# A masked prefix sum of eight sequences: blocks planned from registers, or a gather by a table of units

## The chip, the cores and the metric

The kernel runs on one core of a Trainium2 chip. The metric is the device time of one execution in microseconds, first to last instruction, given as the median of several executions. Lower is better.

## What is computed

```
B, S, D = 8, 8192, 512          # x: 8 x 8192 x 512 fp32, lengths: 8 whole numbers, w: 512 x 512 fp32
mask = pos < lengths
cs = cumsum(x * mask, axis=1)
mid = cs[b, lengths[b] // 2, :]
out = mid @ w                   # 8 x 512
```

Only one row of each cumulative sum is used, so for sequence b the answer is the sum of its first n rows, with n = min(lengths // 2 + 1, lengths), times w. For the lengths of this draw (1138, 5379, 511, 4113, 1809, 7542, 7716, 1140), n is 570, 2690, 256, 2057, 905, 3772, 3859 and 571: 14,680 rows of 2 KB in all, 30.1 MB. They must be read from memory; the arithmetic is small. The lengths are known only on the chip, so the program must decide there which rows it reads.

## The kernel before

The row sum is a matrix product: a block of rows lies in SBUF with 128 partitions, and TensorE multiplies it by a matrix 128 x 8 that has ones in the column of the sequence, adding into `s_ps`. Four such products, each in its own column group of the array, take the four rows that a partition holds; the four groups are added up later by a product with `fold`.

SyncE issues all reads of x, and TensorE must know which of them there are. Each of the two loads all the lengths from memory into registers and works the row counts out there (`counts`, line 80, and the arithmetic of lines 83 to 85). Then come three passes.

- Whole blocks (lines 97 to 115): for each sequence, `whole_blocks` compares n with 512, 1024 and so on, and for each block that is full issues one 1 MB transfer in which every partition gets four consecutive rows, 8 KB. `xt` holds the blocks of two sequences; block k of sequence b waits (line 105) until the block k of sequence b-2 is summed. For this draw there are 26 blocks.
- Remainders (lines 121 to 153): what is left of each sequence, below 512 rows, is read by the binary digits of n: 256 rows (line 129, two rows or 4 KB a partition), 128 rows (line 136, 2 KB a partition), and the last up to 127 rows in a multiple of 32 (line 143). They go into `rem`, and the last piece is multiplied by `mask`, which VectorE makes of the lengths.
- The end: after a closing product (line 254) VectorE copies `s_ps` to SBUF (one copy of 128x512), TensorE folds and transposes it (line 261), VectorE copies, TensorE multiplies by w (line 268), VectorE copies, and four transfers write the output from two queues (lines 156 and 165).

ScalarE's queue loads lengths for VectorE and the whole of w (lines 161 and 162) at the start. GpSimd clears part of `rem` (line 169) and makes two index vectors. VectorE's helper `step` (line 182) runs one operation at a time, each waiting for the one before. Nothing here is reordered by a scheduler: each engine runs its list in the order written.

Of the kernel before, what the change touches and what calls it, by code (L numbers as in the profile page):

```python
# [8 lines left out]
I32 = mybir.dt.int32  # L9
ALU = mybir.AluOpType  # L10
ds = bass.ds
# [4 lines left out]
def kernel(  # L16
# [10 lines left out]


    nc = tc.nc
    ctx.enter_context(nc.allow_non_contiguous_dma(reason="lengths"))  # L30
    B, S, D = x.shape
    G = 4
    BLK = P * G
    NB = S // 2 // BLK
    KC = D // P
    STEP = 32
    xf = x.rearrange("b s d -> (b s) d")
# [12 lines left out]

    xt = sb("xt", [P, 2, NB, G, D])
    rem = sb("rem", [P, B, G, D])
    wt = sb("wt", [P, KC, D])
    lens = sb("lens", [P, 2 * B], I32)
    cnt = sb("cnt", [P, B], I32)
    cap = sb("cap", [P, B], I32)
    row = sb("row", [P, 1], I32)
    mask = sb("mask", [P, B, B])
    sel = sb("sel", [P, 2 * B - 1])
    zero = sb("zero", [1, D])  # L60
    fold_i = sb("fold_i", [P, B], I32)
    fold = sb("fold", [P, B])
# [5 lines left out]
    mf_ps = ps("mf_ps", [P, D])  # L68
    o_ps = ps("o_ps", [P, D])

    s_full = [[sem(f"full{b}_{k}") for k in range(NB)] for b in range(B)]
    s_rem = [[sem(f"rem{b}_{k}") for k in range(3)] for b in range(B)]
    s_free = [sem(f"free{b}") for b in range(B)]
    s_w, s_len, s_out = sem("w"), sem("len"), sem("out")
    s_pool, s_dve, s_pe = sem("pool"), sem("dve"), sem("pe")

    def counts(eng):

        regs = [eng.alloc_register(f"n_{eng.engine.name}_{i}") for i in range(2 * B)]
        eng.load(regs, lens_words)  # L80
        for b in range(B):
            length, n = regs[2 * b], regs[2 * b + 1]
            eng.reg_alu(n, length, 1, ALU.logical_shift_right)
            eng.reg_alu(n, n, 1, ALU.add)
            eng.reg_alu(n, n, length, ALU.min)
        return regs[1::2], regs[0]

    def whole_blocks(eng, n, body, k=0):
        if k < NB:
            with eng.If_cmp(n, BLK * (k + 1), "IS_GE"):  # L90
                body(k)
                whole_blocks(eng, n, body, k + 1)

    DVE_SEL, DVE_MASK = 3, 12

    block = ctx.enter_context(nc.Block(no_gpsimd_drain=True))

    @block.sync
    def _(sp):
        ns, t = counts(sp)  # L100

        def wait_free(b, k):

            if b >= 0:
                with sp.If_cmp(ns[b], BLK * (k + 1), "IS_GE"):  # L105
                    sp.wait_ge(s_free[b], k + 1)
                with sp.Else():
                    wait_free(b - 2, k)

        for b in range(B):  # L110
            def load_block(k):
                wait_free(b - 2, k)
                sp.dma_start(  # L113
                    out=xt[:, b % 2, k],
                    in_=x[b, k * BLK:(k + 1) * BLK].rearrange("(p g) d -> p g d", g=G),
                ).then_inc(s_full[b][k], 16)

            whole_blocks(sp, ns[b], load_block)

        def rows(b, first, count):  # L120
            return xf[ds(sp.snap(first) + b * S, count)]  # L121

        sp.wait_ge(s_pool, 1)
        for b in range(B):
            base = sp.alloc_register(f"base{b}")
            sp.reg_alu(t, ns[b], 256, ALU.bitwise_and)
            with sp.If_cmp(t, 1, "IS_GE"):
                sp.reg_alu(base, ns[b], ~(2 * 256 - 1), ALU.bitwise_and)
                sp.dma_start(  # L129
                    out=rem[:, b, 0:2],  # L130
                    in_=rows(b, base, 256).rearrange("(p g) d -> p g d", g=2),
                ).then_inc(s_rem[b][0], 16)
            sp.reg_alu(t, ns[b], 128, ALU.bitwise_and)
            with sp.If_cmp(t, 1, "IS_GE"):
                sp.reg_alu(base, ns[b], ~(2 * 128 - 1), ALU.bitwise_and)
                sp.dma_start(out=rem[:, b, 2], in_=rows(b, base, 128)).then_inc(s_rem[b][1], 16)  # L136
            sp.reg_alu(t, ns[b], 127, ALU.bitwise_and)
            sp.reg_alu(base, ns[b], ~127, ALU.bitwise_and)

            def load_last(lo, hi):  # L140

                if hi - lo == STEP:
                    sp.dma_start(out=rem[:hi, b, 3], in_=rows(b, base, hi)).then_inc(s_rem[b][2], 16)  # L143
                    return
                mid = (lo + hi) // 2
                with sp.If_cmp(t, mid, "IS_GT"):
                    load_last(mid, hi)
                with sp.Else():
                    load_last(lo, mid)

            with sp.If_cmp(t, 1, "IS_GE"):
                load_last(0, 128)

        sp.wait_ge(s_dve, DVE_MASK + 3)
        for j in range(0, 4, 2):
            sp.dma_start(out=out[:, j * P:(j + 1) * P], in_=o_sb[32 * j:32 * j + B]).then_inc(s_out, 16)
        sp.wait_ge(s_out, 64)

    @block.scalar
    def _(act):  # L160
        act.dma_start(out=lens[:], in_=lens_words.to_broadcast((P, 2 * B))).then_inc(s_len, 16)
        act.dma_start(out=wt[:], in_=w.rearrange("(kc p) d -> p kc d", p=P)).then_inc(s_w, 16)
        act.wait_ge(s_dve, DVE_MASK + 3)
        for j in range(1, 4, 2):
            act.dma_start(out=out[:, j * P:(j + 1) * P], in_=o_sb[32 * j:32 * j + B]).then_inc(s_out, 16)

    @block.gpsimd
    def _(pool):
        pool.memset(rem[:, :, 3], 0.0).then_inc(s_pool, 1)  # L169
        pool.iota(row[:], pattern=[[0, 1]], base=0, channel_multiplier=1)  # L170
        pool.iota(fold_i[:], pattern=[[-1, B]], base=128, channel_multiplier=1).then_inc(s_pool, 1)

    @block.vector
    def _(dve):
        done = 0

        def step(do, *args, **kw):

            nonlocal done
            if done:  # L180
                dve.wait_ge(s_dve, done)
            do(*args, **kw).then_inc(s_dve, 1)  # L182
            done += 1

        step(dve.memset, zero[:], 0.0)
        step(dve.memset, sel[:], 0.0)
        step(dve.memset, sel[:, B - 1:B], 1.0)
        assert done == DVE_SEL
        step(dve.memset, mask[:], 0.0)
        step(dve.memset, o_ps[:, :P], 0.0)  # L190
        dve.wait_ge(s_len, 16)
        step(dve.tensor_scalar, out=cnt[:], in0=lens[:, ::2], scalar1=1, scalar2=None,
             op0=ALU.logical_shift_right)
        step(dve.tensor_scalar, out=cap[:], in0=cnt[:], scalar1=1, scalar2=None, op0=ALU.add)
        step(dve.tensor_tensor, out=cnt[:], in0=cap[:], in1=lens[:, ::2], op=ALU.min)
        step(dve.tensor_scalar, out=cap[:], in0=cnt[:], scalar1=127, scalar2=None,
             op0=ALU.bitwise_and)
        dve.wait_ge(s_pool, 2)
        step(dve.tensor_tensor, out=mask[:].rearrange("p a b -> p (a b)")[:, ::B + 1], in0=cap[:],
             in1=row[:].to_broadcast((P, B)), op=ALU.is_gt)  # L200
        step(dve.tensor_scalar, out=cnt[:], in0=fold_i[:], scalar1=31, scalar2=None,
             op0=ALU.bitwise_and)
        step(dve.tensor_scalar, out=fold[:], in0=cnt[:], scalar1=0, scalar2=None, op0=ALU.is_equal)
        assert done == DVE_MASK
        dve.wait_ge(s_pe, 1)
        step(dve.tensor_copy, out=s_sb[:], in_=s_ps[:])
        dve.wait_ge(s_pe, 2)
        step(dve.tensor_copy, out=mf_sb[:].rearrange("p a b -> p (a b)"), in_=mf_ps[:, :KC * B])
        dve.wait_ge(s_pe, 3)
        step(dve.tensor_copy, out=o_sb[:], in_=o_ps[:, :P])  # L210

    @block.tensor
    def _(pe):
        ns, t = counts(pe)

        def add(j, weights, rows):

            return pe.matmul(s_ps[32 * j:32 * j + weights.shape[-1]], lhsT=weights, rhs=rows,  # L218
                             start=False, stop=False, skip_group_check=True,
                             tile_position=(0, 32 * j))  # L220

        pe.wait_ge(s_dve, DVE_SEL)
# [3 lines left out]
        for b in range(B):  # L226
            one = sel[:, B - 1 - b:2 * B - 1 - b]

            def add_block(k):
                pe.wait_ge(s_full[b][k], 16)  # L230
                for j in range(G):
                    mm = add(j, one, xt[:, b % 2, k, j])
                mm.then_inc(s_free[b], 1)

            whole_blocks(pe, ns[b], add_block)
# [66 lines left out]
```

## Time and profile before

| what | value |
|---|---|
| median of 3 executions | 101.29 us (100.38 to 101.92) |
| span of the profiled execution | 100.6 us |
| TensorE busy | 58.3 us |
| VectorE busy | 3.9 us |
| GpSimd busy | 4.0 us |
| bytes moved | 31.48 MB, mean 313 GB/s |
| 26 whole blocks, 1024 KB each | 12.8 us median from issue to landing |
| w, 1024 KB | 5.4 us from issue to landing |

The page gives time in microseconds from the first instruction. "SPq" is SyncE's queue, "ACTq" ScalarE's; a DMA row of a timeline shows how long the queue took to issue a transfer, not how long the data travelled. "PEld" is TensorE's load of weights. In a table of stages, "DMA share" is the mean busy share of the 16 DMA engines and the last number is what they moved. [...]

### The profile page before, as it was taken

The page shows a single profiled execution, that of the slowest core. Times are in us where ns is not written, and L with a number is a line of the kernel's source. Part 1 is how long each engine was busy: PE and PEld are TensorE (multiplying, and loading weights), DVE is VectorE, ACT ScalarE, POOL GpSimd, SP SyncE. Part 2 cuts the span into 40 slices and gives each one's busy share as a digit, 9 for nine tenths or more (in the row PEclk, how much of TensorE's full clock was granted, in tenths as well). Part 3 has the DMA queues.
Part 4 walks back from the last instruction along what each step waited for, and adds up shares of the span by engine and source line. Part 5 has one row for each costly group of instructions (what it writes and reads, how often), then busy time and mean ns, then how long its engine had stood idle before and what let it go on. Part 6 is the DMA issues. An engine that isn't in the chain of part 4 may idle for free.

```text
span 100.6 us, 1017 instructions
## 1 busy us (share of the span) xinstructions
PE 58.3 (58%) x296; PEld 8.3 (8%) x296; DVE 3.9 (4%) x15; POOL 4.0 (4%) x7
## 2 busy tenths in 40 slices
PE   0006177744763954199444767744755796996820
PEld 0000000000000100010000000000000111113700
DVE  3520000000000000000000000000000000002010
POOL 7800000000000000000000000000000000000000
PEclk9999999998555699755999555596555569998555
DMA  0836999999999999999999999999999995100000
GB/s 2 270 148 195 427 427 430 430 420 420 427 420 417 427 423 417 414 417 414 427 420 420 423 423 423 410 420 423 420 281 290 328 283 136 34 0 0 0 7 0
DMA packets 5786, 31.48 MB, mean 313 GB/s; under 512 B 816, under 2 KB 848, under 8 KB 2448
## 3 DMA queue, kind: packets, MB, share of 16 engines
q1 hardware_dynamic: 5072, 30.29, 76.3%
q10 hardware_dynamic: 704, 1.07, 3.2%
q8 instruction: 5, 0.08, 0.3%
q14 instruction: 5, 0.04, 0.1%
HBM read 31.33 MB, written 0.02 MB: 312 GB/s over the span
## 4 chain that ended last, share of the span: by engine, by line
DMA 41%; SPq 31%; issue 13%; PE 9%; DVE 1%
DMA xt<-in_x_dram 25%; DMA rem<-in_x_dram 16%; SPq L113 10%; SPq L143 6%; SPq L80 5%; PE s_ps L218 5%; SPq L129 3%; PE o_ps L268 2%; PE mf_ps L261 2%; SPq L105 1%; SPq L136 1%; PE s_ps L254 1%; SPq L90 1%; DVE s_sb L182 1%; SPq L121 1%
## 5 line engine op out<-in xcount | busy, mean ns | idle before, releaser
L218 PE MATMUL s_ps<-xt,sel 128*8 128x512 f32 x208 | 42.6, 905 | 28.6 <-DMA xt<-in_x_dram 23.4
L218 PEld LDWEIGHTS s_ps<-xt,sel 128*8 128x8 f32 x208 | 3.7, 91 | 67.5 <-DMA xt<-in_x_dram 58.0
L218 PE MATMUL s_ps<-rem,mask 128*8 128x512 f32 x14 | 8.0, 670 | 0.8 <-issue 0.8
L218 PE MATMUL s_ps<-rem,sel 128*8 128x512 f32 x18 | 6.6, 643 | 0.1
L224 PE MATMUL s_ps<-zero 1*32 1x512 f32 x8 | 1.9, 1056 | 7.3 <-issue 7.3
L182 DVE COPY s_sb<-s_ps 128x512 f32<-128x512 f32 x1 | 0.7, 692 | 85.8 <-PE s_ps L254 85.8
L169 POOL MEMSET rem<- 128x4096 f32 x1 | 3.5, 3512 | 0.5 <-SPq L40 0.5
L261 PE MATMUL mf_ps<-fold,s_sb 128*128 128x8 f32 x8 | 1.7, 340 | 0.8 <-DVE s_sb L182 0.8
L268 PE MATMUL o_ps<-wt,mf_sb 128*8 128x128 f32 x32 | 1.9, 416 | 0.3 <-DVE mf_sb L182 0.3
L261 PEld LDWEIGHTS mf_ps<-fold,s_sb 128*128 128x128 f32 x8 | 1.6, 298 | 1.7 <-DVE s_sb L182 1.7
L218 PEld LDWEIGHTS s_ps<-rem,mask 128*8 128x8 f32 x14 | 1.0, 97 | 6.0 <-issue 4.1
L268 PEld LDWEIGHTS o_ps<-wt,mf_sb 128*8 128x8 f32 x32 | 1.1, 126 | 0.7 <-DVE mf_sb L182 0.4
L254 PE MATMUL s_ps<-zero 1*32 1x512 f32 x8 | 1.1, 600 | 0.0
L218 PEld LDWEIGHTS s_ps<-rem,sel 128*8 128x8 f32 x18 | 0.6, 87 | 3.3 <-DMA rem<-in_x_dram 3.1
L182 DVE TENSOR_SCALAR cnt<-lens 128x8 int32<-128x8 int32 x1 | 0.8, 822 | 1.3 <-DMA lens<-in_lengths_dram 1.3
L224 PEld LDWEIGHTS s_ps<-zero 1*32 1x32 f32 x8 | 0.2, 136 | 7.3 <-issue 7.3
L182 DVE MEMSET zero<- 1x512 f32 x1 | 0.5, 485 | 1.1 <-PEq L286 1.1
L182 DVE COPY o_sb<-o_ps 128x128 f32<-128x128 f32 x1 | 0.3, 291 | 2.0 <-PE o_ps L268 2.0
L182 DVE TENSOR_SCALAR cap<-cnt 128x8 int32<-128x8 int32 x2 | 0.3, 172 | 0.1
L182 DVE COPY mf_sb<-mf_ps 128x32 f32<-128x32 f32 x1 | 0.2, 192 | 1.8 <-PE mf_ps L261 1.8
L254 PEld LDWEIGHTS s_ps<-zero 1*32 1x32 f32 x8 | 0.2, 102 | 0.9 <-issue 0.9
L182 DVE TENSOR_TENSOR mask<-cap,row 128x8 f32<-128x8 int32 x1 | 0.2, 173 | 0.1
(12 smaller groups left out, 1.6 us busy)
## 6 DMA issues: line engine op xcount, KB each, us to landing
xt<-in_x_dram SPq DMA_DIRECT2D x26, 1024.0 KB, 12.8
rem<-in_x_dram SPq DMA_DIRECT2D x3, 512.0 KB, 22.5
wt<-in_w_dram ACTq DMA_DIRECT2D x1, 1024.0 KB, 5.4
rem<-in_x_dram SPq DMA_DIRECT2D x3, 256.0 KB, 22.1
rem<-in_x_dram SPq DMA_DIRECT2D x3, 128.0 KB, 16.2
rem<-in_x_dram SPq DMA_DIRECT2D x4, 64.0 KB, 21.3
out_dram<-o_sb SPq DMA_DIRECT2D x2, 4.0 KB
out_dram<-o_sb ACTq DMA_DIRECT2D x2, 4.0 KB
```

Source lines behind the costliest of these rows:

```text
L80: eng.load(regs, lens_words)
L90: with eng.If_cmp(n, BLK * (k + 1), "IS_GE"):
L113: sp.dma_start(out=xt[:, b % 2, k], in_=x[b, k * BLK:(k + 1) * BLK].rearrange("(p g) d -> p g d", g=G),).then_inc(s_full[b][k], 16)
L129: sp.dma_start(out=rem[:, b, 0:2], in_=rows(b, base, 256).rearrange("(p g) d -> p g d", g=2),).then_inc(s_rem[b][0], 16)
L143: sp.dma_start(out=rem[:hi, b, 3], in_=rows(b, base, hi)).then_inc(s_rem[b][2], 16)
L169: pool.memset(rem[:, :, 3], 0.0).then_inc(s_pool, 1)
L182: do(*args, **kw).then_inc(s_dve, 1)
L218: return pe.matmul(s_ps[32 * j:32 * j + weights.shape[-1]], lhsT=weights, rhs=rows, start=False, stop=False, skip_group_check=True, tile_p ...
L224: pe.matmul(s_ps[32 * j:32 * j + 32], lhsT=zero[:, :32], rhs=zero[:], start=True, stop=False, skip_group_check=True, tile_position=(0, 32 ...
L254: mm = pe.matmul(s_ps[32 * j:32 * j + 32], lhsT=zero[:, :32], rhs=zero[:], start=False, stop=True, skip_group_check=True, tile_position=(0 ...
L261: mm = pe.matmul(mf_ps[:, kc * B:(kc + 1) * B], lhsT=s_sb[:, kc * P:(kc + 1) * P], rhs=fold[:], start=True, stop=True)
L268: mm = pe.matmul(o_ps[32 * j:32 * j + B, :P], lhsT=mf_sb[:, kc], rhs=wt[:, kc, j * P:(j + 1) * P], start=(kc == 0), stop=(kc == KC - 1), t ...
```

## The change

The blocks and remainders give way to one list. x is seen as an array of units of four rows (8 KB), `xu`, and the units that are wanted are numbered through all sequences. A table `idx` says for each place of the list which unit it is; one indirect transfer on GpSimd's queue takes 128 places, one for each partition, into one of R = 8 slots of `xt`.

What is read without a table goes ahead and behind: the first 512 rows of sequences 0 and 1 (FRONT, two plain transfers of 1 MB on SyncE's queue, wanted for any lengths), and the first 128 rows of sequences 6 and 7 (BACK, two plain transfers of 256 KB behind the list). w is read in four parts behind these. The list has (length >> 3) + 1 units of a sequence less what FRONT or BACK hold of it: here 15 + 545 + 64 + 515 + 227 + 911 + 933 + 111 = 3,321 units, 26 gathers, the last with 121 places filled. Places past the end get an index out of bounds and are left out by the transfer; the slots are cleared beforehand by ScalarE, so that such a place holds no garbage the first time.

- VectorE, from lengths on one partition: per-sequence counts, a running sum (a scan), and the steps of the index; TensorE spreads the row to all partitions (one product with ones, `bc_ps`); then a comparison, a product and a reduction give `idx`, for the first C1 = 8 gathers and then for the other 57 that the largest lengths could need. After this VectorE makes `wf`, `wc` and `wb`, the weights 128 x 8 for each row of a unit, which hold the mask.
- GpSimd: gather 0 after `idx0`; then it loads the number of units into a register, waits for the whole table, and issues gather after gather, with a comparison and a branch between; gather c waits until ScalarE has cleared its slot (c below 8) or TensorE has summed gather c-8.
- TensorE: FRONT, then four products a gather with `wc`, then BACK, then the fold and the product with w. Copies at the end go in four quarters. The closing product is gone.

The core of the diff (setup of constants and names left out):

```diff
-    xt = sb("xt", [P, 2, NB, G, D])
-    rem = sb("rem", [P, B, G, D])
+    xt = sb("xt", [P, R, U * D])
+    xf = sb("xf", [P, FRONT, U, D])
+    xb = sb("xb", [P, BACK, D])
...
-        ns, t = counts(sp)
...
+    def sync(sp):
+        sp.dma_start(out=xf[:, 0], in_=x[0, :P * U].rearrange("(p u) d -> p u d", u=U)).then_inc(
+            s_front[0], 16)
+        sp.dma_start(out=xf[:, 1], in_=x[1, :P * U].rearrange("(p u) d -> p u d", u=U)).then_inc(
+            s_front[1], 16)
+        sp.wait_ge(s_dve, marks["out"])
...
-        act.dma_start(out=lens[:], in_=lens_words.to_broadcast((P, 2 * B))).then_inc(s_len, 16)
-        act.dma_start(out=wt[:], in_=w.rearrange("(kc p) d -> p kc d", p=P)).then_inc(s_w, 16)
+        act.dma_start(out=lens[:], in_=lens_words).then_inc(s_len, 16)
+        for k in range(R):
+            act.memzero(xt[:, k]).then_inc(s_zero, 1)
...
+        def gather(c):
+            if c < R:
+                pool.wait_ge(s_zero, c + 1)
+            else:
+                pool.wait_ge(s_done, c - R + 1)
+            pool.indirect_dma_start(
+                out=xt[:, c % R], out_offset=None, in_=xu,
+                in_offset=bass.IndirectOffsetOnAxis(ap=idx[:, c:c + 1], axis=0),
+                bounds_check=B * UB - 1, oob_is_err=False,
+            ).then_inc(s_full[c % R], 16)
...
+        pool.wait_ge(s_dve, marks["idx0"])
+        gather(0)
+        pool.load(n, total[:])
+        pool.wait_ge(s_dve, marks["idx"])
+        pool.br("gp_1")
+        with nc.body("gp_tail", valid_engines=[pool.engine]):
+            for k in range(BACK):
+                pool.dma_start(out=xb[:, k], in_=x[B - BACK + k, :P]).then_inc(s_back[k], 16)
+            for k in range(KC):
+                pool.dma_start(out=wt[:, k], in_=w[k * P:(k + 1) * P]).then_inc(s_w[k], 16)
...
+        def table(a, e):
+            n = e - a
+            step(tt, out=ge[:, a:e], in0=q[:, a:e].unsqueeze(2).to_broadcast((P, n, B)),
+                 in1=bc_ps[:, :B].unsqueeze(1).to_broadcast((P, n, B)), op=ALU.is_ge)
+            step(tt, out=z[:, a:e, :B], in0=ge[:, a:e],
+                 in1=bc_ps[:, B:2 * B].unsqueeze(1).to_broadcast((P, n, B)), op=ALU.mult)
+            step(dve.tensor_reduce, out=idx[:, a:e], in_=z[:, a:e], axis=AX.X, op=ALU.add)
...
+        def weights(a, e):
...
+            step(tt, out=wc[:, a:e], in0=early[:, a:e],
+                 in1=ge[:, a:e].unsqueeze(2).to_broadcast((P, n, U, B)), op=ALU.mult)
...
+        for k in range(KC):
+            step(dve.tensor_copy, out=s_sb[:, k * P:(k + 1) * P], in_=s_ps[:, k * P:(k + 1) * P])
...
+        def chunk(c):
+            pe.wait_ge(s_full[c % R], 16 * (c // R + 1))
+            for u in range(U):
+                mm = add(u, wc[:, c, u], xt[:, c % R, u * D:(u + 1) * D])
+            mm.then_inc(s_done, 1)
...
+            for k in range(KC):
+                pe.wait_ge(s_dve, marks["mf"] - KC + k + 1)
+                pe.wait_ge(s_w[k], 16)
```

## The prediction, made before the changed kernel ran

> **What bounds the kernel now.** I read the slices of the page first, to see when the DMA engines work:
>
> ```profile
> DMA  0836999999999999999999999999999995100000
> GB/s 2 270 148 195 427 427 430 430 420 420 427 420 417 427 423 417 414 417 414 427 420 420 423 423 423 410 420 423 420 281 290 328 283 136 34 0 0 0 7 0
> ```
>
> They are full from 10 to 84 us: the transfers of x are the bound, not TensorE (58.3 us busy of 100.6). But there are poor stretches at both ends. The table of stages sizes them:
>
> ```profile
> 0.00:2.50 2.50, 0.00 (x0) 0.00 (x0) 0.89 (x5) 1.76 (x5) 1.00 0.01 2
> 2.50:5.00 2.50, 0.00 (x0) 0.00 (x0) 1.24 (x4) 2.21 (x3) 1.00 0.86 267
> 5.00:7.50 2.50, 0.18 (x4) 0.19 (x8) 0.61 (x4) 0.00 (x0) 1.00 0.40 154
> 7.50:10.00 2.50, 1.75 (x8) 0.02 (x3) 0.00 (x0) 0.00 (x0) 1.00 0.61 197
> 10.00:72.00 62.00, 37.01 (x188) 3.42 (x192) 0.00 (x0) 0.00 (x0) 0.75 1.01 421
> 72.00:84.00 12.00, 8.53 (x34) 0.97 (x33) 0.00 (x0) 0.00 (x0) 0.57 1.02 298
> 84.00:88.00 4.00, 3.71 (x16) 0.70 (x18) 0.00 (x0) 0.00 (x0) 1.00 0.18 56
> 88.00:101.00 13.00, 7.11 (x56) 3.02 (x52) 1.18 (x3) 0.00 (x0) 0.68 0.01 1
> ```
>
> The last two numbers are DMA share and GB/s. Whole blocks (8 KB a partition) move at 421 GB/s, remainders (2 and 4 KB) at 298 with the engines just as busy. The head, up to 10 us, moves 1.5 MB; the tail from 84 us moves almost nothing. The timeline says why the head is poor:
>
> ```profile
> 1.34 0.45 ACTq L162 DMA_DIRECT2D wt<-in_w_dram  x1
> 3.66 0.82 DVE L182 TENSOR_SCALAR cnt<-lens 128x8 int32<-128x8 int32 x1 [1.33 <-DMA lens<-in_lengths_dram]
> 7.20 12.37 SPq L113 DMA_DIRECT2D xt<-in_x_dram  x8
> ```
>
> SyncE issues no x before 7.20, since it is loading lengths to registers; only w runs until then. VectorE has the lengths at 3.66. And the chain that ended last gives the end:
>
> ```profile
> 71.56 16.25 DMA rem<-in_x_dram
> 87.85 2.68 PE s_ps L218 x8
> 90.53 1.03 PE s_ps L254 x8
> 91.59 0.70 DVE s_sb L182
> 92.34 1.71 PE mf_ps L261 x8
> 94.07 0.20 DVE mf_sb L182
> 94.32 1.94 PE o_ps L268 x32
> 96.28 0.29 DVE o_sb L182
> ```
>
> From the last landing (87.85) to the end of the last copy (96.57) are 8.7 us of products and copies in series, and then 4.0 us for output and close.
>
> **What the Trainium skill says.** (1) "DMA: Bandwidth & Descriptors", section "Issuing engines are not separate DMA queues": all transfers share the same 16 engines, whichever engine starts them. So the move to GpSimd brings no bandwidth by itself. The trace agrees as far as it goes: at 421 GB/s the share is already 1.01. (2) The same page, "Latency and other measured facts": first byte after some 0.6 us when SP or ACT issue, some 1 us when GpSimd does, since its cores write the descriptors. No row here shows a GpSimd transfer. (3) "SBUF — State Buffer", "SBUF: two separate sides": such descriptors can't be written while VectorE holds the port that it shares with GpSimd. Not shown here either. (4) "ScalarE: Activation LUTs", "What ACT_TABLE_LOAD costs": 186 + 0.833 N ns for an activation with immediates, 2.66 us for a table switch; no activation runs in the trace of before.
>
> **The change part by part.**
>
> *Bytes.* Front 2.10 MB, gathers 3,321 x 8,192 = 27.21 MB, back 0.52, w 1.05: 30.9 MB against 31.48. Nothing is won by the amount. What changes is the packet (the rest of each sequence now in 8 KB units) and when the stream starts and ends.
>
> *Head.* SyncE reaches its first transfer without a register load, at about 1.0 us (ScalarE issues at 0.91). How long from issue to stream? Before, x was issued at 7.20, and by 10.0 0.197 x 2.5 = 0.49 MB had gone, or 1.2 us at 421: it started at 8.8, 1.6 us after issue. So front streams from 2.6 and is through at 2.6 + 2.10/0.421 = 7.6.
>
> Is the first table ready by then? Lengths land at 3.66. Before that VectorE has 12 memsets (0.48 us for the 512-wide one, about 0.13 a step for the others, from 1.12 on: to 2.9) and five operations on constants; a dependent step of before takes 0.20 us (0.17 busy), and the very first such operation took 0.82: to 4.5 at worst. Then l8, max, scan, subtract: 4 x 0.2 = 5.3; one product to spread it, 0.5 with its waits (an mf_ps product lasts 340 ns): 5.8; three table steps of 64 to 72 elements, 0.22 each: 6.5. Gather 0 is issued, first byte after 1 to 2 us (the page's 1 us, and twice that for index reading, which no row prices): 7.5 to 8.5. I take a hole of 0.5 us (0 to 1.5). Behind it gather 0 streams 2.5 us, to 10.6. Meanwhile four steps (0.8) and the big table: 456, 456 and 513 elements at about 1 ns each (512 took 485 ns in the memset) plus 0.07: 1.7 us. The table stands at 9.1, gather 1 flows from 10.1 to 11.1: another hole of 0.5 at most. The register load on GpSimd lies beside these steps.
>
> *The gathers.* Each moves 1.05 MB: 2.49 us at 421. This is the question of the case: does GpSimd issue one in less? The trace has no such row. From below, 1 us, the page's first byte; from above, the 2.0 us that the same page ("Anatomy of one DMA — SWDGE (gpsimd) path") gives as the whole fixed part of a transfer. 128 index reads and bounds checks add to it, unpriced. I take 1.5 us: hidden, GpSimd then runs up to 8 slots ahead and waits for TensorE. 25 gathers after the first: 26.16/0.421 = 62.1 us, from 11.1 to 73.2.
>
> *Waits that the gathers add.* ScalarE clears slots: 186 + 0.833 x 2048 = 1.89 us each, from 1.3 + 2.7 = 4.0 on, so slot c is clear at 4.0 + 1.89(c + 1), slot 7 at 19.1; the stream needs gather 7 at 10.6 + 6 x 2.49 = 25.5. Hidden under the gathers before. All else on GpSimd stands behind this wait, but the seven gathers' lead covers it. TensorE's release: four products take 1.05 us (the xt groups of x4), less than 2.49; hidden. The weights `wc` (1,824 elements twice, 1.9 us each, ready near 16 us) could lock GpSimd out for 2 us; by then it is a few transfers ahead. TensorE can't sum gather 0 before about 11 us (`w0`), and catches up at 1.05 against 2.49. All these at nothing.
>
> *Tail.* Back and w (2 KB a partition) at the remainders' 298 GB/s: 1.57/0.298 = 5.3 us, to 78.5; landing 0.8 later (a 1 MB block landed 4.96 us after issue: 1.6 start + 2.5 stream + 0.8): 79.3. Beside it: the last gather is there at 74.0, back at 75.8, its eight products 0.9, four quarter copies at 0.29 (the 128x128 copy) with fold products and small copies running behind them, about 1.9: 78.6. So w ends last, narrowly. Then four products (0.45), the copy (0.3), gaps (0.15): 80.2, and 4.0 for output and close: 84.2. The median of before is 0.7 above its profiled span: 84.9.
>
> Against before: head 10 us with 1.5 MB becomes 11.1 with 3.15 MB; the 298 GB/s stretch shrinks from some 3.6 MB to 1.6; 8.7 us of products after the last byte become 0.9. Forecast 85.
>
> **The rivals.** *GpSimd becomes the bound.* For it: the bracket of its price is open at the top. Then the last gather is through at 9.1 + 25G, six plain transfers take about 1 us each to issue, 2.4 us to landing, 4.9 to the end: 22.4 + 25G. G = 2.5 gives 85, 3.0 gives 97, and 3.4 gives 107, slower than before. Against: the page's 2.0 us is well below 2.49. Chance of some bound within 86 to 99: 0.13; of slower, 107: 0.09.
>
> *The gathered stream is slower than a plain one.* The page's table for GpSimd transfers has 341 GB/s for a lone 1 MB and 425 for 16 MB. At 341 the 27.2 MB take 79.8 us and not 64.6: 100, about no change; at 385, 70.7: 91. For it: scattered units, descriptors fetched from memory. Against: the packets stay 8 KB and eight transfers are in the queue. 0.15, most of it near 91.
>
> *The start is late* (table 3 us later, or a cleared slot on the path): 88. 0.08. Forecast 0.55.
>
> **How the numbers follow.** The low end: no holes (-1.0), w and back at 421 (-1.6), a quicker close (-1): 81. The high end takes the slow stream and most of the mild GpSimd bound: 97. Beyond it are the slower rival and a little of "same". Faster by 2% (below 99.3) 0.86, same 0.05, slower 0.09.
>
> **What would show it.** Right: x moving from about 2.6 us, slices at 410 to 430 GB/s from 11 to 73, GpSimd's gathers waiting for TensorE's sums, the wait for w last before o_ps. Wrong: GB/s well below 400 with DMA share near 1 (slow stream); gaps in the DMA share with GpSimd never waiting (GpSimd's bound); a hole between 8 and 15 us (late table or clearing).

## The result, and the profile after

| | before | after |
|---|---|---|
| median | 101.26 us | 97.28 us (96.47 to 98.0) |
| ratio to before, 95% interval | | 0.9605 (0.9532 to 0.9677) |
| profiled span | 100.6 us | 95.5 us |

Faster by 4%, in the direction forecast, but 12.4 us above the 84.9 that the forecast's sum came to, and just outside its range (81 to 97). Some executions fall into a slower state, here the 98.0, and the ratios leave them out.

One count has to be put right first. The change's section and the prediction give the list 3,321 units in 26 gathers. The sequence of length 7542 has no BACK, so it has 943 units and not 911: the list is 3,353 units, 27.47 MB, in 27 gathers, the last with 25 places filled.

The slices of the changed kernel, to be laid beside those of before:

```profile
DMA  2894799999999999999999999999999995000000
GB/s 31 353 412 120 288 353 374 422 425 429 412 436 429 422 401 436 419 412 432 425 412 425 429 412 422 432 412 419 432 422 415 393 389 208 22 0 3 3 10 0
```

x now moves from 2 us on, and from about 10 us the engines stay nearly full to the end of the list. Two things are worse than forecast: the hole in the fourth slice, with thin slices behind it, and six slices at the end in which almost nothing moves. The table of stages (last three columns: granted TensorE clock, DMA share and GB/s) sizes them:

```profile
0.00:5.00 5.00, 2.36 (x16) 0.58 (x16) 2.79 (x21) 3.53 (x3) 1.56 (x10) 1.00 0.55 195
5.00:7.50 2.50, 0.60 (x2) 0.50 (x2) 1.85 (x11) 2.50 (x2) 0.07 (x1) 1.00 1.00 423
7.50:10.00 2.50, 0.59 (x2) 0.49 (x2) 2.14 (x7) 2.50 (x3) 1.12 (x1) 1.00 0.39 79
10.00:12.50 2.50, 2.37 (x12) 0.44 (x16) 2.29 (x7) 2.50 (x3) 1.84 (x2) 1.00 0.89 344
12.50:15.00 2.50, 2.46 (x16) 0.15 (x8) 2.47 (x2) 2.50 (x2) 1.89 (x3) 1.00 1.00 364
15.00:20.00 5.00, 1.43 (x12) 0.23 (x16) 2.21 (x4) 2.26 (x2) 4.02 (x4) 1.00 0.99 401
20.00:72.00 52.00, 33.42 (x168) 2.40 (x160) 0.00 (x0) 0.00 (x0) 22.07 (x25) 0.67 1.01 423
72.00:84.00 12.00, 7.39 (x48) 1.06 (x48) 0.01 (x1) 0.00 (x0) 0.00 (x0) 0.65 0.69 270
```

From 20 to 72 us the gathered stream moves 423 GB/s, as fast as the plain blocks of before (421). GpSimd's timeline settles the case's main question (start, duration, and in brackets how long GpSimd was idle before and what ended that by the profile):

```profile
7.42 1.19 POOL L151 DMA_INDIRECT xt<-in_x_dram,idx  x1 [5.00 <-DVE row L184]
10.36 1.02 POOL L151 DMA_INDIRECT xt<-in_x_dram,idx  x1 [1.74 <-DVE wf L184]
11.68 0.99 POOL L151 DMA_INDIRECT xt<-in_x_dram,idx  x1 [0.30 <-issue]
...
15.57 1.78 POOL L151 DMA_INDIRECT xt<-in_x_dram,idx  x1 [0.30 <-ACT xt L132]
...
27.30 0.99 POOL L151 DMA_INDIRECT xt<-in_x_dram,idx  x1 [1.50 <-PE s_ps L286]
```

A gather takes 0.99 us of GpSimd and 0.30 to the next: 1.29, about half of the 2.49 that its bytes take. Later ones wait for TensorE to free a slot, so GpSimd is not the bound once the list runs. The chain that ended last shows where the time is instead:

```profile
77.74 2.56 PE s_ps L286 x16
80.29 2.60 issue
82.89 1.08 PE s_ps L286 x16
...
84.97 0.30 DVE s_sb L184
85.27 0.62 issue
85.89 1.67 PE mf_ps L331 x8
87.55 1.87 PE o_ps L337 x32
89.42 0.02 issue
89.45 0.29 DVE o_sb L184
```

The last packet of w is through at 82.07 by the trace, but the products with w start at 87.5 and don't wait for it. Ahead of BACK's products (line 286 at 82.89) TensorE stands still for 2.60 us and waits for nothing that the profile shows; before the fold (line 331) again, 0.62. The second wait begins inside the fold, behind the load of its first weights:

```profile
84.34 0.29 PEld L331 LDWEIGHTS mf_ps<-fold,s_sb 128*128 128x128 f32 x1 [0.90 <-DVE s_sb L184]
85.89 1.57 PEld L331 LDWEIGHTS mf_ps<-fold,s_sb 128*128 128x128 f32 x7 [1.26 <-issue]
```

At the very end a wait of SyncE's queue has grown. The kernel before, then the changed one (columns: us in all, times, longest):

```profile
SPq L297 <- PEq L297: 1.2, 2, 1.0
SPq L387 <- PEq L387: 3.2, 2, 2.7
```

The releaser named is the engine that came last to a barrier by the profile. The trace's own instructions show what held it: a drain of GpSimd from 91.90 that lasts 2.77 us. The same drain takes 0.04 us in the kernel before.

### The profile page after: what moved, and what is told of

It is laid out like the page before. It is cut to its first block, busy times and chain, and to the rows that moved or that the text cites. A ratio compares the mean times of both kernels' runs of the same rounds, so it can differ in the third digit from the quotient of the medians.

```text
span 95.5 us, 890 instructions
## 1 busy us (share of the span) xinstructions
PE 54.1 (57%) x308; PEld 8.8 (9%) x308; DVE 15.9 (17%) x56; ACT 15.8 (17%) x9; POOL 32.6 (34%) x43
## 4 chain that ended last, share of the span: by engine, by line
DMA 53%; ACT 17%; PE 12%; issue 9%; DVE 2%; POOL 1%; ACTq 1%; POOLq 0%; SPq 0%
DMA xt<-in_x_dram,idx 53%; ACT xt L132 15%; PE s_ps L286 8%; PE o_ps L337 2%; PE mf_ps L331 2%; ACT L132 1%; DVE s_sb L184 1%; POOL xt L151 1%; ACTq L130 1%; DVE o_sb L184 0%; POOLq L151 0%; POOLq L171 0%; ACTq L387 0%; SPq L46 0%
## 5 line engine op out<-in xcount | busy, mean ns | idle before, releaser
L286 PE MATMUL s_ps<-xt,wc 128*8 128x512 f32 x216 | 42.5, 877 | 24.1 <-DMA xt<-in_x_dram,idx 24.1
L151 POOL DMA_INDIRECT xt<-in_x_dram,idx x27 | 27.7, 1027 | 33.8 <-PE s_ps L286 23.7
L132 ACT ACTIVATE xt<-xt 128x2048 uint32<-128x2048 uint32 x8 | 14.5, 1895 | 0.0
L184 DVE COPY s_sb<-s_ps 128x128 f32<-128x128 f32 x4 | 1.2, 292 | 66.8 <-PE s_ps L286 66.7
L286 PEld LDWEIGHTS s_ps<-xt,wc 128*8 128x8 f32 x216 | 3.4, 89 | 64.0 <-DMA xt<-in_x_dram,idx 62.0
L286 PE MATMUL s_ps<-xf,wf 128*8 128x512 f32 x16 | 3.6, 1051 | 1.7 <-DVE wf L184 1.7
L184 DVE TENSOR_TENSOR wc<-early,ge 128x256 f32<-128x256 f32 (+1 forms) x2 | 2.5, 1244 | 0.1
L184 DVE TENSOR_TENSOR early<-v,b_ps 128x256 f32<-128x256 f32 (+1 forms) x2 | 2.5, 1237 | 0.1
L167 POOL DMA_DIRECT2D wt<-in_w_dram x4 | 2.2, 575 | 0.0
L165 POOL DMA_DIRECT2D xb<-in_x_dram x2 | 1.2, 595 | 0.0
(45 smaller groups left out, 12.4 us busy)
```

The costliest lines, as they stand in the source:

```text
L132: act.memzero(xt[:, k]).then_inc(s_zero, 1)
L151: pool.indirect_dma_start(out=xt[:, c % R], out_offset=None, in_=xu, in_offset=bass.IndirectOffsetOnAxis(ap=idx[:, c:c + 1], axis=0), boun ...
L165: pool.dma_start(out=xb[:, k], in_=x[B - BACK + k, :P]).then_inc(s_back[k], 16)
L167: pool.dma_start(out=wt[:, k], in_=w[k * P:(k + 1) * P]).then_inc(s_w[k], 16)
L286: return pe.matmul(s_ps[32 * j:32 * j + B, cols], lhsT=weights, rhs=rows, start=False, stop=False, skip_group_check=True, tile_position=(0 ...
```

## The experiments

Theory after the comparison: the miss at the end is (a) TensorE fetching the code of its end, which lies in front of the gathers' code and is jumped back to, and (b) GpSimd's drain, long because it has issued transfers. At the head, (c) the table comes late for the stream. Rivals: TensorE waits there for the transfers behind the list; the drain belongs to the program's end; the slots' clearing or GpSimd holds the stream.

**One early drain.** In GpSimd's end, behind the last issue:

```diff
                 pool.dma_start(out=wt[:, k], in_=w[k * P:(k + 1) * P]).then_inc(s_w[k], 16)
+            pool.drain()
```

> The changed kernel, with one drain of GpSimd written behind its last transfer issue (about 67 us), and nothing else. Theory: the 2.77 us drain of GpSimd at the close is paid once, by the first drain after descriptor work, and can be paid while the transfers run; then the close (from the output copy's end at 89.7) falls from 5.8 to about 3.1 us and the time from 97.3 to about 94.6. Rival: the price belongs to the program's end whatever ran before; then the time stays at 97.3.

Measured: 94.83 us, ratio 0.9415 (0.9331 to 0.95), 2.45 us less. The early drain runs from 65.3 to 84.1 us, beside the transfers and until 1.8 us after the last packet of w (82.2), and the wait at the close is gone:

```profile
SPq L388 <- PEq L388: 0.7, 2, 0.5
```

So the price is that of the first drain behind the transfers, and it can be paid where nothing waits for GpSimd.

**TensorE's list straight.** The branches go, and the end's code follows behind the 27th gather:

```diff
-                pe.br_cmp(n, P * c, f"pe_go{c}", "pe_tail", "IS_GT")
...
+        for c in range(27):
+            if c == C1:
+                pe.wait_ge(s_dve, marks["w"])
+            chunk(c)
```

> The changed kernel, with TensorE's list written out straight for 27 gathers, the end following without a branch (right only for lists of 27 gathers, as here; GpSimd keeps its branches). Theory: the 2.60 us without work behind the last gather's products, and the 0.62 us before the fold, are instruction fetch after the jump back to the end's code; both vanish, the end comes 3 us sooner: 94.3. Rival: TensorE waits there for the transfers behind the list; then the gap stays and so does 97.3.

Measured: 92.66 us, 0.9126 (0.9022 to 0.9231): 4.6 less, more than expected. The chain that ended last:

```profile
78.19 4.29 PE s_ps L286 x32
82.48 0.02 issue
82.51 0.30 DVE s_sb L184
...
84.65 0.18 DVE mf_sb L184
84.83 0.04 issue
84.87 0.72 PE o_ps L335 x16
```

No gap: BACK's products follow the last gather's at once. The trace's packets bear the theory out: the changed kernel fetches a 16 KB block of code at 79.7 and another at 83.3 us, and here the last comes at 74.2. And since TensorE has its code, the fold runs behind the quarter copies as they end, and half of the products with w behind the copies of the fold: from the first copy to the last product 3.1 us here, 5.4 in the changed kernel. The code wait had also undone the overlap that the quarters are for; how much of the 2.3 us is that, the hint's section below says. The rival is out: the transfers are the same.

**A transfer of GpSimd in the kernel before.**

```diff
-        act.dma_start(out=wt[:], in_=w.rearrange("(kc p) d -> p kc d", p=P)).then_inc(s_w, 16)
+        pool.dma_start(out=wt[:], in_=w.rearrange("(kc p) d -> p kc d", p=P)).then_inc(s_w, 16)
```

> The kernel before, with w's one plain transfer moved from ScalarE's queue to GpSimd's. Theory: any transfer issued by GpSimd makes its drain at the close long; from 101.3 to about 104 with a drain of about 2.7 us. Rival: only indirect transfers, or many of them, do; then about 101.3 with a drain of 0.04 us as before.

Measured: 101.23 us, ratio 0.9997 (0.9958 to 1.0037). The theory in that form fell: one plain transfer leaves the close as it was. The drain itself lasts 0.13 us here and 0.04 in the kernel before (the 0.2 that the next expectation gives for one transfer is too much). Open between number and kind, so:

**The same with 32 transfers.** In place of ScalarE's one:

```diff
+        for k in range(KC):
+            for j in range(8):
+                pool.dma_start(out=wt[:, k, j * 64:(j + 1) * 64],
+                               in_=w[k * P:(k + 1) * P, j * 64:(j + 1) * 64]).then_inc(s_w, 16)
```

> The kernel before, with w read by GpSimd in 32 plain transfers of 128 rows of 256 bytes. Theory now: the closing drain of GpSimd costs by the number of its transfers (2.77 us after 33, 2.60 after 31, 0.2 after one, so some 82 ns each): about 2.7 us after 32, and 101.3 becomes 104. Rival: only indirect transfers make it long; 0.2 us and 101.3.

Measured: 106.45 us, 1.0495 (1.0398 to 1.0592). The wait at the close is back:

```profile
SPq L300 <- PEq L300: 3.6, 2, 2.6
```

The drain lasts 2.67 us after 32 plain transfers, 2.77 after 33 (changed kernel), 2.60 after 31 (next experiment). With 0.04 us after none and 0.13 after one (four times as many rows as in one of the 32), it goes by the number of transfers, at some 82 ns each, and not by kind. The time grew by 5.2 us and so by more than that: w's megabyte now moves from 6.0 to 33.3 us, beside x, and not from 2.7 to 6.4, ahead of it, and the last packet of x ends at 90.36 and not at 87.83.

**BACK at the head.**

```diff
+        for k in range(BACK):
+            sp.dma_start(out=xb[:, k], in_=x[B - BACK + k, :P]).then_inc(s_back[k], 16)
```

with its products behind FRONT's, and a small product of zeros as TensorE's signal at the end.

> The changed kernel, with BACK's two transfers issued by SyncE right behind FRONT and summed there, and one small product of zeros as the signal at the end. Theory: the engines have nothing to move from 7.9 to 9.3 us, so 0.52 MB fit there for little, the last gather lands as before or up to 0.5 us later, and the end loses BACK's 1.08 us of products: 96.3. Rival A: the head's stream delays gather 0 by the whole 1.2 us that 0.52 MB take: 97.4. Rival B: the end waits for w, which then lands 1.2 us sooner: 96.1, with a wait for w in front of the last products.

Measured: 97.32 us, 0.9664 (0.9572 to 0.9755): no gain, where 96.3 was expected. The hole was filled at no cost, as the theory says: from 7.5 to 10 us 272 GB/s and not 79, and gather 25's last 8 KB packet ends at 76.20 (76.19 in the changed kernel), so rival A, whose 97.4 is near, had the wrong reason. But the end still waits for the code:

```profile
78.00 3.60 PE s_ps L286 x16
81.60 0.95 issue
82.55 0.18 PE s_ps L328
82.73 2.56 issue
85.29 0.21 PE s_ps L328
...
85.87 1.87 PE mf_ps L332 x8
```

Two waits now, one on each side of the first half of the zero product: the code comes in two blocks, and the second is what the end waits for. The trace shows two fetches of 16 KB in this stretch, at 79.8 and 83.1 us (79.7 and 83.3 in the changed kernel), and so the fold starts at 85.87, as in the changed kernel (85.89), with BACK's products gone.

**A hint of the branch.** This keeps the branches, and so serves every list:

```diff
-                pe.br_cmp(n, P * c, f"pe_go{c}", "pe_tail", "IS_GT")
+                b = pe.br_cmp(n, P * c + 1, "pe_tail", f"pe_go{c}", "IS_LT")
+                if c > 1:
+                    b.branch_hint(to_tail)
             with nc.body(f"pe_go{c}", valid_engines=[pe.engine]):
+                to_tail = pe.mark_branch_hint_location() if c + 1 < C else None
                 chunk(c)
```

> The changed kernel with its branches, and one thing more: at the head of every gather's products TensorE is told of the branch to the end's code, so that the code can be fetched ahead. Theory: the wait for code behind the last products (2.60 us, and 0.62 before the fold) is known ahead and hides behind the wait for data; the time falls toward that of the straight list, 92.7 (taken: 93). Rival: with room for few blocks of code the hinted block is driven out again before it is used, or drives out the next gathers' code; then the gap stays and so does 97.3.

Measured: 91.86 us, 0.9069 (0.899 to 0.9148), as good as the straight list. The chain has no gap there:

```profile
78.06 3.02 PE s_ps L286 x32
81.07 0.02 issue
81.10 0.30 DVE s_sb L184
```

The one fetch of code that is left in this stretch, at 80.1 us, lies beside the last products.

Not all of the gain is code. The clock that TensorE was granted differs too, as the pages' row of it says, in tenths of full speed for 40 slices (changed kernel, BACK at the head, hint):

```profile
PEclk9999999995555975579556955597596559755555
PEclk9999999985555965556957955596559755795555
PEclk9999999955557955557955597556956955599955
```

In the changed kernel the clock is at half speed from 82.5 us on, with the hint at full speed from 79.4 to 86.2. BACK at the head tells the two apart, since there the code is at hand when the copies begin and the clock is at half speed from 85.6 on: from the first copy to the last product it takes 4.1 us, against 5.4 in the changed kernel and 3.1 with the straight list (full speed from 82.1 to 85.5) and with the hint. So some 1.3 us of that stretch are code (0.6 of gap, 0.7 of lost overlap) and 1.0 goes with the clock. With the 2.6 us ahead of BACK the wait for code cost 3.9 us. The chains' ends (from the start of the last two gathers' products to the last product with w) are 4.3 us shorter with the straight list and 5.6 with the hint; what is over 3.9 goes with the clock, in one profiled execution each. Why the clock fell as it did, no run shows.

**The three together, twice.**

> The changed kernel with the hint, the early drain of GpSimd and BACK at the head together; it stays right for every list of lengths. If the three are independent: 97.3 less 4.3 (hint), 2.5 (drain), 1.1 (BACK's products): 89.4. If the hint does nothing: about 94.8, since BACK at the head alone brought nothing beside the wait for code.

> The kernel with hint, early drain and BACK at the head once more, unchanged, as the one to compare the two gathers ahead with on the same chip: 90.2.

Measured: 90.24 us, 0.888 (0.8785 to 0.8976), and 89.53, 0.8856 (0.875 to 0.8962), 0.8 and 0.1 above the 89.4 of three independent terms.

> The changed kernel with TensorE's list straight for 27 gathers (right only for lists of that many), the early drain and BACK at the head. If the three terms are independent: 97.3 less 4.6, 2.5 and 1.1: 89.1, and w, landing near 81.5, is what the last products wait for, or nearly. If the terms hide each other (w is a floor): about 90.2, the straight list and the drain alone.

Measured: 89.54 us, 0.8818 (0.873 to 0.8907), between its two expectations. The end's chain has no wait for w either, so w is no floor.

**The clearing of the slots.** It goes, and GpSimd's wait for it:

```diff
-        for k in range(R):
-            act.memzero(xt[:, k]).then_inc(s_zero, 1)
```

> The changed kernel without ScalarE's clearing of the slots and without the wait for it (right for lists of at least 1,024 units, as here: every slot is filled whole before it is used in part). Theory (as predicted): the clearing lies beside the gathers ahead of it and costs nothing: 97.3. Rival: the chain that ended last runs through it to 17.3 us, 15% of the span, so it holds the stream back; then gathers 5 and on land sooner and the time falls by 0.5 to 2 us.

Measured: 97.64 us, 0.9652 (0.9532 to 0.9772): no change. In the page's chain of the changed kernel this line has 15% of the span:

```profile
DMA xt<-in_x_dram,idx 53%; ACT xt L132 15%; PE s_ps L286 8%; PE o_ps L337 2%; PE mf_ps L331 2%; ACT L132 1%; DVE s_sb L184 1%; POOL xt L151 1%; ACTq L130 1%; DVE o_sb L184 0%; POOLq L151 0%; POOLq L171 0%; ACTq L387 0%; SPq L46 0%
```

That share is misleading. The profile infers what released an engine from the times of semaphore events, and a slot's clearing happened to end just ahead of an issue. No gather was held by it: gathers 5, 6 and 7 are issued at 15.57, 17.65 and 18.94 us with the clearing and at 15.54, 17.64 and 18.94 without. Without clearing the stream is as thin from 10 to 15 us (377 and 360 GB/s), so it isn't the cause of that either.

**Two gathers ahead of the whole table**, on top of the three, with both loops beginning at gather 2:

```diff
         gather(0)
+        gather(1)
         pool.load(n, total[:])
```

> The kernel with hint, early drain and BACK at the head, and one thing more: gathers 0 and 1 both go out ahead of the register load and of the whole table, since the first table holds eight. Gather 1's descriptors then start at about 8.7 us and not at 10.4. Theory: the stream between 8 and 20 us (360 to 377 GB/s against 422 later) is thin since GpSimd has only one gather out, and gathers land 1 to 1.5 us sooner to the end: 1 to 1.5 us below the kernel without it in the same call. Rival: the thin stretch comes of something else that runs then (ScalarE's clearing, the making of descriptors itself); then all lands as before, within 0.4 us.

Measured: 88.19 us, 0.8742 (0.8629 to 0.8855), against 89.53 without it: 1.3 less. The intervals of the ratios overlap; the single times that they are made of (87.97 to 88.25, and 88.97 to 89.95) do not. GpSimd's second issue starts at 8.90 and not at 10.35, and gather 26's last packet ends at 77.66 and not at 78.31, so the head gave 0.65 us and not 1 to 1.5. The rest of the difference between the two profiled executions lies in the products of the last two gathers, 2.07 us here and 3.35 without, at a granted clock of 1.00 and of 0.55 (78 to 80 us). The stretch from 10 to 15 us stays thin (351 and 370 GB/s): only part of that is one gather being out alone.

> The kernel with hint, early drain and two gathers ahead, but BACK where the change has it, behind the list. If BACK at the head is worth its 1.08 us of products at the end: 89.3, a ratio to the kernel before of about 0.885 against 0.874 with it. If its products now lie hidden or the head pays for it: 88.2 and 0.874 as with it.

Measured: 89.15 us, 0.8889 (0.8789 to 0.899) against 0.8742 with BACK at the head. The stream ends at the same time (last packet 77.64 and 77.66), so BACK at the head costs nothing, and with the code there in time it looks worth up to the 1.1 us that it was taken for. That isn't firm: the intervals overlap, and the clock at the end differs here too (0.50 and 0.98 from 76 to 78 us). The kernel with all four, written for any lengths but run here with these alone, is the fastest of the general ones: 12.6% less than before.

## Why the prediction was wrong

It said 84.2 us of span, and 84.9 for the median; measured were 95.5 and 97.3.

- **The bound, the gathers, GpSimd's pace: right.** 1.29 us a gather (1.5 taken, 1 to 2 the bracket, and 2.49 available); 423 GB/s against 421; both rivals on this fell. The waits costed at nothing cost nothing: the clearing (1.89 us a slot, as estimated) by the experiment; the weights by the timeline. The Trainium skill ("SBUF — State Buffer", "SBUF: two separate sides") says that a VectorE operation with two inputs in SBUF shuts a GpSimd operation that reads SBUF out of the port they share until it ends, and the trace agrees: the gather at 15.57 took 1.78 us and not 0.99, while VectorE's long product of `wc` ran to 16.48. GpSimd was ahead, so nothing came of it. No run removed that product.
- **The head: right in kind, 2.5 us too short.** The first table was ready at 6.47 (6.5 predicted), but from there to the first packet of gather 0 it took 2.84 us (9.31) and not 1 to 2; gather 0 then took 4.1 us to flow, and the third was through at 18.6 and not 16.1. With the nearly steady pace from there, that shift lasts to the end. The 1 us that the Trainium skill gives ("DMA: Bandwidth & Descriptors", "Latency and other measured facts") is too little here: from GpSimd's start at 7.42 to the first packet are 1.9 us. "A hole of 0.5" was the step (1.4 us, from 7.93 to 9.31); the thin stretch behind it was not foreseen at all. Of the 2.5, 1.2 are the later first packet (9.31 and not 8.1), and the rest lies in the thin stretch.
- **The last landing: 78.75 and not 74.0.** Of the 4.75, 2.5 are the head's; 1.0 is the 27th gather that the miscount left out. The rest, about 1.2, is the longer time from a last packet to the products that wait for it (1.5 us for gather 25 and not 0.8) and the pace (2.50 us a gather and not 2.48, over 23 gathers 0.5).
- **The tail: the step "so w ends last, narrowly" failed.** From the last landing to the last product it had 5.75 us; measured are 10.7: the 27th gather's products 1.5, code 2.6, BACK 1.1, copies 1.3, code 0.6, fold 1.7, product with w 1.9. w itself was through at 82.07, when TensorE had not yet begun BACK, so the products with w waited for TensorE's own work and not for w. The 3.2 of waits for code stood nowhere in the prediction, and they took 0.7 of overlap between copies and fold with them; straight list and hint gave back 4.6 and 5.4, a better clock at the end included. A reason to ask was there beforehand: the Trainium skill, "Runtime: NRT & Kernel Launch", section "Instruction fetch mechanics", says that a taken branch out of the two pages of code at hand waits for a fetch. The prediction asked of each added wait what stands behind it, and of the branches nothing. The trace agrees: a 16 KB block of code is fetched at 79.71 (1.38 us) and one at 83.34 (1.19 us), and TensorE goes on 1.8 and 1.4 us after they are in, at the ends of the two waits.
- **The close: "4.0 for output and close" failed**, at 5.8 us, by GpSimd's drain of 2.77, which the move of 33 transfers to its queue had added. Shown by the early drain (2.45 us back) and by 32 transfers put into the kernel before.
- **The offset: 1.1 us.** Taken was the median of before less its profiled span, 0.7, which are two different executions. Of one execution the time lies about 1.8 us above its span, before and after (101.05 and 99.3, 97.31 and 95.5).

In sum 4.75 for the landing, 4.9 for the tail (10.7 less 5.75), 1.8 for the close and 1.05 for the offset, less 0.1 in the last copy: 12.4, which is what was missed (97.3 less 84.9). The rival "the start is late" was true as well, with 2.5 of these; of the two that made the difference, code and drain, neither was among the rivals.

What stays open: why the stream is thin (344 to 377 GB/s at a DMA share of 0.9 to 1.0) from 10 to 15 us. It is not the clearing, and only in part the lone gather. The trace says where the time goes: 48 of the 384 packets of 8 KB of gathers 0 to 2 took more than 0.4 us, up to 1.3, where the median is 0.31; in the 24 gathers behind them 4 did. Over 16 engines the excess is 1.25 us. With two gathers ahead it is 0.86, against 1.55 in the same kernel without, and that is about the 0.65 us that it gained. The slow packets belong to the gathers whose first packet came soonest after their issue (1.9, 2.2 and 3.9 us for gathers 0 to 2, 5.3 for gather 3); what makes them slow, no run shows.

## What to carry to other kernels

Where runtime branches choose what an engine runs, look where the code of the end lies: a jump back just when the last data land puts an instruction fetch on the path, and a hint ahead of the branch or code in a straight line takes it off. When transfers move to GpSimd's queue, count them and let GpSimd drain early, behind its last issue, rather than at the close. Filling a hole or taking work off the tail shows only once what ends last there is gone: BACK at the head gave nothing alone, and perhaps 1 us when the code was there.

## What was not expected of the hardware

- GpSimd's closing drain: about 82 ns for each transfer that it has issued (0.04, 0.13, 2.60, 2.67 and 2.77 us after 0, 1, 31, 32 and 33, gathers and plain ones alike); written behind the last issue it ran beside the transfers and left nothing for the close.
- GpSimd's issue is cheap: 0.99 us for a gather of 128 rows of 8 KB, about 0.58 for a plain 128 rows of 2 KB; but 1.9 us from the issue's start to the first packet (1.8 and 1.4 for the first plain transfer of w in the two experiments with the kernel before).
- A wait for code cost more than its own length: 3.2 us of gaps and 0.7 of lost overlap. What came back beyond these 3.9 (4.6 us with the straight list and 5.4 with the hint, in all) lies, as far as the profiled executions show, with the clock that TensorE was granted at the end.
